# Rope's cosine product on VectorE, late steps of the q chain one by one, and two in three of the second head's exponential sums on VectorE

## The chip, the cores and the metric

The kernel runs on one core of a Trainium2 chip. The time is device microseconds (us) of one execution, the median of three runs: 2183.52 us for the kernel before. The engines are named as the profile names them: PE (TensorE; PEld is its loading of weights), DVE (VectorE), ACT (ScalarE), POOL (GpSimd) and SP (SyncE, which issues the transfers). Each engine works through its own queue in order; an instruction that waits holds up all that stands behind it in that queue.

## The reference, cut to what matters

```python
for i in range(DEPTH):                       # DEPTH = 2 layers, 1040 positions x 1024 channels
    hn = rmsnorm(h, norm_w[i])
    proj = einsum("bld,de->ble", hn, w_in[i])
    (u_pool, g_pool, u_fft, g_fft, xbc, z, dt_raw, q, k, v, g_attn) = split(proj, points)
    y_pool = multiscale_pool(...) * silu(g_pool)
    y_fft = fourier_mix(...) * silu(g_fft)
    y_ssd = ssd_mixer(...)
    y_att = gqa_axial(q, k, v, ...) * silu(g_attn)
    h = h + einsum("ble,ed->bld", concatenate([y_pool, y_fft, y_ssd, y_att]), w_out[i])

def gqa_axial(q, k, v, q_norm_w, k_norm_w, cos, sin):   # 8 query heads, 2 key heads, 64 wide
    q = rope2d(rmsnorm(q, q_norm_w), cos, sin)
    k = rope2d(rmsnorm(k, k_norm_w), cos, sin)
    s = einsum(q, k) * scale
    p = softmax(s, axis=-1)
    return einsum(p, v)
```

The change lies in the rope of q and k, and in the denominators of the softmax.

## The kernel before

Everything is kept with channels on the 128 partitions and positions along the columns. The 1040 positions are cut into three chunks `CH` of 348, 346 and 346 columns (332 for the first in layer 1), and the keys into nine tiles `KTS` of 116 (112 for the last).

**Projections.** `proj` computes one tile of 128 output channels: for each chunk 8 x 3 matmuls (`mm3`, lines 133 to 135: high part times high, high times low, low times high), with a `yield` after every second of the eight groups, so four steps a chunk (`PC = 4`). It then calls `evac` on the PSUM tile. If `evac` is a generator, its first part runs before the last `yield` of the chunk; with `QS = 1` all that is left of it runs at once at the start of the next step, ahead of the next chunk's matmuls. Weights come in by `wraw` (line 198) and are split in `split`: ACT writes the high part (129), DVE the low part (130).

**The q and k chain, `qk_chunk`, the body of `evac` for these tiles.** ACT copies the projection out of PSUM (528) and squares it (530), then a `yield`; PE sums the squares over each head (533), `rstd` makes the inverse root in three ACT and three DVE instructions (139 to 146), DVE multiplies with it (535) and swaps neighbours (537), SP loads the cosines (539) and sines (540), POOL multiplies with the cosines (541), DVE multiplies the swapped copy with the sines (542) and adds the two (543). `att_q` then writes the result's high and low parts (ACT 585, DVE 586), `att_kv` those of the key tile (558 to 560). There are 30 such chunks: 2 layers x (1 key tile + 4 query tiles) x 3 chunks. Their small tiles come from a ring of four (`smq`).

**Attention.** `att_max` finds an upper bound of each query's scores: 27 or so matmuls per head (605) and a DVE maximum of each (606), in some 20 steps; the negated maxima are brought across by POOL's memset (609), PE transposes (616) and ACT copies (618). `att_main` goes through three chunks of queries with nine key tiles each; `score` does, for the two heads `e` = 0, 1 of a tile `t`, two matmuls (634, 635), the exponential on ACT (637), and adds the exponentials of successive key tiles up on POOL (644 for key tiles 0 and 1, 646 for the others). `weigh` multiplies with v (656), `divide` turns the sums into the quotients (665 to 671). An exponential's tile (`pf`, 14 buffers) is free when both `weigh` and its sum have read it.

**What runs beside what.** `weave` interleaves generators: each has a nominal number of steps, and the next step is taken from the one that is least far along. For query tile `t` it weaves `att_main(t)` (38 + 12 steps), `att_q(t+1)` and `att_max(t+1)` (20 + 12 steps) and a part of `fill`, a chain of the other projections and their side work (`FO`; "D" is the SSD step sizes `ssd_dt`, lines 708 to 744, and `pool_group` works in lines 695 and 696). Ahead of that stand, in program order, `prenorm`, `att_kv`, whose two streams (the key and the value projection) take four steps by turns, and `fft_tables` (lines 392 to 420: loads of `fw`, DVE additions 407 and 411, matmuls 415). After attention come the output projections and the SSD scans, which the change doesn't touch.

The order within each engine's queue is not the program's: a planner sets it when the program is built, from the program's order and from its own estimate of when each instruction could start. So instructions of neighbouring steps pass each other.

Of the kernel before, what the change touches and what calls it, by code (L numbers as in the profile page):

```python
# [14 lines left out]
ALU = mybir.AluOpType  # L15
# [37 lines left out]
def hybrid_trunk(ctx: ExitStack, tc: tile.TileContext, io, out, depth=DEPTH):  # L53
    nc = tc.nc
# [28 lines left out]
    PC = 8 // GK  # L83
# [3 lines left out]
    LS = 38  # L87
    QS = 1
    OS = (7, 8)
# [62 lines left out]
    def vec(l, col, n=1):  # L152
        return vecs[:, l * NV + col:l * NV + col + n]
# [47 lines left out]
    def proj(s, w, evac, cols=128, ch=CH):  # L201
        for ci, (c0, cw) in enumerate(ch):
            p = ps("mm")
            for k in range(8):
                mm3(p[:cols, :cw], *w[k], s.hh[k][:, c0:c0 + cw], s.hl[k][:, c0:c0 + cw], k == 0, k == 7)
                if k % GK == GK - 1 and k < 7:
                    yield
            late = evac(ci, c0, cw, p[:cols, :cw])
            late = late if isgenerator(late) else iter(())
            if QS:  # L210
                next(late, None)
                yield
            for _ in late:
                pass
            if not QS:
                yield

# [308 lines left out]
    def qk_chunk(l, s, wcol, c0, cw, p):  # L526
        raw = sm("q")
        nc.scalar.copy(raw[:, :cw], p)
        sq = sm("q")
        nc.scalar.activation(sq[:, :cw], raw[:, :cw], AF.Square)  # L530
        yield
        ss = ps("xx")
        nc.tensor.matmul(ss[:, :cw], blk, sq[:, :cw], start=True, stop=True)
        rs = rstd(ss[:, :cw], cw, 64, "q")
        nc.vector.scalar_tensor_tensor(raw[:, :cw], raw[:, :cw], vec(l, wcol), rs[:, :cw], op0=ALU.mult, op1=ALU.mult)
        sw = sm("q")
        nc.vector.stream_shuffle(sw[:, :cw], raw[:, :cw], [i ^ 1 for i in range(32)])
        cos, sin = sm(), sm()
        nc.sync.dma_start(cos[:, :cw], io["cosT"][:, c0:c0 + cw])
        nc.sync.dma_start(sin[:, :cw], io["sinT"][:, c0:c0 + cw])  # L540
        nc.gpsimd.tensor_tensor(raw[:, :cw], raw[:, :cw], cos[:, :cw], op=ALU.mult)
        nc.vector.tensor_tensor(sw[:, :cw], sw[:, :cw], sin[:, :cw], op=ALU.mult)
        nc.vector.tensor_tensor(raw[:, :cw], raw[:, :cw], sw[:, :cw], op=ALU.add)
        return raw

    def att_kv(l, s):
# [16 lines left out]
        for _ in CH:  # L563
            for g in streams:
                yield from islice(g, PC)
        yield from chain(*streams)
# [54 lines left out]
    def att_main(l, s, t):  # L621
# [5 lines left out]
        def score(c0, cw, k):  # L627
# [4 lines left out]
            for e in range(2):  # L632
# [5 lines left out]
                pfs.append(pf)  # L638
            for e, pf in enumerate(pfs):
                if k == 0:  # L640
                    first[e] = pf
                elif k == 1:
                    accs[c0, e] = phase["p"].tile([128, 348], F32, name=nm("acc"), tag="acc", bufs=NACC)
                    nc.gpsimd.tensor_tensor(accs[c0, e][:n, :cw], first[e][:n, :cw], pf[:n, :cw], op=ALU.add)
                else:
                    nc.gpsimd.tensor_tensor(accs[c0, e][:n, :cw], accs[c0, e][:n, :cw], pf[:n, :cw], op=ALU.add)  # L646
            return pfs
# [332 lines left out]
    for l in range(depth):  # L980
# [29 lines left out]
        phase["spare"] = SPARE[1]  # L1010
        run(weave((chain(att_q(l, s, 0), att_max(l, s, 0)), 3 * PC + 17), (islice(fill, FN[0] * PC), FN[0] * PC)))
        for t in range(4):
# [5 lines left out]
            if t < 3:  # L1018
                run(weave((att_main(l, s, t), LS + 3 * PC), (chain(*side), 20 + 3 * PC), (islice(fill, n), n)))
        d0, d1, d2 = [hidden() for _ in range(3)]  # L1020
# [134 lines left out]
```

## Time and profile before

| | |
|---|---|
| median of 3 runs | 2183.52 us (2173.6 to 2186.84) |
| the profiled execution | 2183.98 us, of which the span is 2181.9 us |
| PE busy | 2002.1 us, 92% of the span |
| DVE busy | 1323.7 us, 61% |
| ACT busy | 1004.6 us, 46% |
| POOL busy | 642.0 us, 29% |
| granted TensorE clock, mean | 0.964 |

A profile shows one execution. A row of the timeline gives start, duration, engine, line, operation, the tile written and those read, how many instructions are merged in it, and in brackets how long the engine stood idle before it and what ended that. A row of the waits gives an engine and line, what it waited for, the total, the number of times and the longest. In a row of the windows, PEclk is the granted clock as a share of 2.4 GHz.

### The profile page before, as it was taken

What the parts mean: (1) busy time and instruction counts of PE and PEld (TensorE: products, weight loads), DVE (VectorE), ACT (ScalarE), POOL (GpSimd) and SP (SyncE); (2) the same over time, 40 slices, a digit from 0 to 9 for tenths busy, and PEclk for the clock granted to TensorE, in tenths of its full rate; (3) what the DMA queues carried; (4) which work ended last, traced back from release to release, by engine and by line L of the source; (5) the groups of instructions that cost most, each with busy time, mean ns of one, the idle gap of its engine ahead of it and who ended that gap; (6) DMA issues with size and microseconds to landing.
All of it is one profiled execution on the core that took longest, in us unless ns stands there. A gap on an engine that the chain in (4) does not pass through costs nothing. (4 is left out here: it accounts for less than half of the span.)

```text
span 2181.9 us, 33618 instructions
## 1 busy us (share of the span) xinstructions
PE 2002.1 (92%) x11868; PEld 1755.1 (80%) x11868; DVE 1323.7 (61%) x2614; ACT 1004.6 (46%) x2191; POOL 642.0 (29%) x642
## 2 busy tenths in 40 slices
PE   6699999989999999988976999999999999988888
PEld 5498888867899868877864988888778997878778
DVE  6373535558566355689864735256576554466996
ACT  5335254444443456346443353444435425463562
POOL 3005235135131220245220142441442304112550
PEclk9799999999999999999997999999999999999999
DMA  4321222113224478776743212121223335776666
GB/s 131 103 86 61 59 66 74 36 56 95 94 81 137 126 217 267 195 186 187 223 125 108 88 59 68 64 63 34 76 81 99 124 113 149 246 231 179 176 190 188
DMA packets 170374, 269.48 MB, mean 124 GB/s; under 512 B 21522, under 2 KB 117334, under 8 KB 170206
## 3 DMA queue, kind: packets, MB, share of 16 engines
q1 hardware_dynamic: 167550, 258.01, 39.0%
q0 software_dynamic: 2656, 9.33, 1.7%
q8 instruction: 93, 1.52, 0.3%
q14 instruction: 75, 0.61, 0.1%
HBM read 189.27 MB, written 73.77 MB: 121 GB/s over the span
## 5 line engine op out<-in xcount | busy, mean ns | idle before, releaser
L133 PE MATMUL psmm<-big,wh 128*128 128x346 f32 (+2 forms) x1920 | 639.8, 333 | 27.0 <-ACT sms L334 9.2
L134 PE MATMUL psmm<-big,wh 128*128 128x346 f32 (+2 forms) x1920 | 629.7, 328 | 7.7 <-DVE big L130 4.0
L135 PE MATMUL psmm<-big,wl 128*128 128x346 f32 (+2 forms) x1920 | 626.3, 326 | 2.0 <-DVE wl L130 2.0
L646 POOL TENSOR_TENSOR acc<-acc,pf 116x346 f32<-116x346 f32 (+4 forms) x336 | 343.9, 1048 | 531.6 <-ACT pf L637 531.5
L133 PEld LDWEIGHTS psmm<-big,wh 128*128 128x128 f32 x1920 | 367.9, 192 | 62.2 <-issue 21.7
L134 PEld LDWEIGHTS psmm<-big,wh 128*128 128x128 f32 x1920 | 368.2, 192 | 19.5 <-DVE big L130 8.4
L135 PEld LDWEIGHTS psmm<-big,wl 128*128 128x128 f32 x1920 | 368.3, 192 | 6.3 <-DVE wl L130 2.6
L130 DVE TENSOR_TENSOR wl<-wr,wh 128x512 fp32r<-128x512 f32 x232 | 182.8, 792 | 215.2 <-ACT wh L129 214.2
L129 ACT CAST wh<-wr 128x512 fp32r<-128x512 f32 (+1 forms) x236 | 145.0, 616 | 270.9 <-PE psmm L134 216.7
L133 PE MATMUL psy<-big,wh 128*128 128x346 f32 (+2 forms) x672 | 224.1, 334 | 0.0
L134 PE MATMUL psy<-big,wh 128*128 128x346 f32 (+2 forms) x672 | 223.1, 332 | 1.1 <-POOL big L182 0.7
L135 PE MATMUL psy<-big,wl 128*128 128x346 f32 (+2 forms) x672 | 219.2, 326 | 0.0
L606 DVE TENSOR_REDUCE mx<-psy 128x1 f32<-128x346 f32 (+3 forms) x272 | 132.8, 512 | 56.1 <-PE psy L605 55.4
L637 ACT ACTIVATE pf<-psy 116x346 f32<-116x346 f32 (+4 forms) x288 | 125.6, 457 | 80.3 <-PE psy L635 77.2
L656 PE MATMUL pspv<-pf,vt 116*64 116x346 f32 (+5 forms) x864 | 160.6, 463 | 0.0
L133 PEld LDWEIGHTS psy<-big,wh 128*128 128x128 f32 x672 | 129.9, 193 | 10.9 <-issue 8.8
L134 PEld LDWEIGHTS psy<-big,wh 128*128 128x128 f32 x672 | 130.0, 193 | 8.5 <-DVE big L130 2.8
L135 PEld LDWEIGHTS psy<-big,wl 128*128 128x128 f32 x672 | 130.3, 194 | 1.3 <-issue 0.8
L606 DVE TENSOR_REDUCE mx<-pssc 128x1 f32<-128x346 f32 (+3 forms) x136 | 69.9, 514 | 69.3 <-PE pssc L605 68.4
L337 DVE TENSOR_TENSOR sms<-sms,psmm 128x346 f32<-128x346 f32 (+2 forms) x128 | 65.1, 511 | 73.7 <-PE psmm L135 43.8
L656 PEld LDWEIGHTS pspv<-pf,vt 116*64 116x64 f32 (+1 forms) x864 | 58.6, 136 | 61.5 <-issue 24.0
L634 PE MATMUL psy<-big,big 128*116 128x346 f32 (+4 forms) x288 | 95.8, 334 | 8.1 <-DVE mx L606 7.2
(285 smaller groups left out, 3331.3 us busy)
## 6 DMA issues: line engine op xcount, KB each, us to landing
wr<-w SPq DMA_DIRECT2D x248, 256.0 KB
hd<-sms SPq DMA_DIRECT2D x112, 173.0 KB
sms<-hd SPq DMA_DIRECT2D x112, 173.0 KB
bb<-csd SPq DMA_DIRECT2D x40, 338.0 KB
md<-big SPq DMA_DIRECT2D x24, 520.0 KB
gd<-sms SPq DMA_DIRECT2D x64, 173.0 KB
big<-gd SPq DMA_DIRECT2D x16, 520.0 KB
big<-md SPq DMA_DIRECT2D x16, 520.0 KB
```

The source lines that it names most:

```text
L129: nc.scalar.copy(hi, src)
L130: nc.vector.tensor_tensor(lo, src, f(hi), op=ALU.subtract)
L133: nc.tensor.matmul(out_ps, ah, bh, start=start, stop=False)
L134: nc.tensor.matmul(out_ps, ah, bl, start=False, stop=False)
L135: nc.tensor.matmul(out_ps, al, bh, start=False, stop=stop)
L337: nc.vector.tensor_tensor(ht, ht, p[:, :cw], op=ALU.add)
L606: nc.vector.tensor_reduce(mx[:qn, q, e, ci:ci + 1], p[:qn, :cw], axis=AX.X, op=ALU.max)
L634: nc.tensor.matmul(p[:n, :cw], k1[:, k0:k0 + n], s1[e][:, cs], start=True, stop=False)
L637: nc.scalar.activation(pf[:n, :cw], p[:n, :cw], AF.Exp, scale=0.125)
L646: nc.gpsimd.tensor_tensor(accs[c0, e][:n, :cw], accs[c0, e][:n, :cw], pf[:n, :cw], op=ALU.add)
L656: nc.tensor.matmul(hold["pv"][64 * e:64 * e + 64, :cw], s.vt[:n, k, v, :], pfs[e][:n, :cw], start=(k == 0), stop=(k == len(KTS) - 1))
```

## The change

The generator in `proj` hands on every `yield` of `evac` as a step of its own, and `qk_chunk` has two more: one after `rstd`, one at its end. The nominal step numbers grow with that (6 more for the 3 chunks of a query tile; in `att_kv` the key stream takes six steps by turns with four of the value stream). The cosine product moves from POOL to DVE, and so do the sums of head `e` = 1 for the key tiles `k` = 1, 2, 4, 5, 7 and 8.

```diff
-    QS = 1
...
             late = evac(ci, c0, cw, p[:cols, :cw])
             late = late if isgenerator(late) else iter(())
-            if QS:
-                next(late, None)
-                yield
-            for _ in late:
-                pass
-            if not QS:
-                yield
+            next(late, None)
+            yield
+            yield from late
...
         rs = rstd(ss[:, :cw], cw, 64, "q")
+        yield
         nc.vector.scalar_tensor_tensor(raw[:, :cw], raw[:, :cw], vec(l, wcol), rs[:, :cw], op0=ALU.mult, op1=ALU.mult)
...
-        nc.gpsimd.tensor_tensor(raw[:, :cw], raw[:, :cw], cos[:, :cw], op=ALU.mult)
+        nc.vector.tensor_tensor(raw[:, :cw], raw[:, :cw], cos[:, :cw], op=ALU.mult)
         nc.vector.tensor_tensor(sw[:, :cw], sw[:, :cw], sin[:, :cw], op=ALU.mult)
         nc.vector.tensor_tensor(raw[:, :cw], raw[:, :cw], sw[:, :cw], op=ALU.add)
+        yield
         return raw
...
         for _ in CH:
-            for g in streams:
-                yield from islice(g, PC)
+            for g, n in zip(streams, (PC + 2, PC)):
+                yield from islice(g, n)
...
             for e, pf in enumerate(pfs):
+                eng = nc.vector if e == 1 and k % 3 else nc.gpsimd
                 if k == 0:
                     first[e] = pf
                 elif k == 1:
                     accs[c0, e] = phase["p"].tile([128, 348], F32, name=nm("acc"), tag="acc", bufs=NACC)
-                    nc.gpsimd.tensor_tensor(accs[c0, e][:n, :cw], first[e][:n, :cw], pf[:n, :cw], op=ALU.add)
+                    eng.tensor_tensor(accs[c0, e][:n, :cw], first[e][:n, :cw], pf[:n, :cw], op=ALU.add)
                 else:
-                    nc.gpsimd.tensor_tensor(accs[c0, e][:n, :cw], accs[c0, e][:n, :cw], pf[:n, :cw], op=ALU.add)
+                    eng.tensor_tensor(accs[c0, e][:n, :cw], accs[c0, e][:n, :cw], pf[:n, :cw], op=ALU.add)
...
-        run(weave((chain(att_q(l, s, 0), att_max(l, s, 0)), 3 * PC + 17), (islice(fill, FN[0] * PC), FN[0] * PC)))
+        run(weave((chain(att_q(l, s, 0), att_max(l, s, 0)), 3 * PC + 6 + 18), (islice(fill, FN[0] * PC), FN[0] * PC)))
...
-                run(weave((att_main(l, s, t), LS + 3 * PC), (chain(*side), 20 + 3 * PC), (islice(fill, n), n)))
+                run(weave((att_main(l, s, t), LS + 3 * PC), (chain(*side), 20 + 3 * PC + 6), (islice(fill, n), n)))
```

## Rows read from the trace of the kernel before

**Rows 1.** The page's first part: busy time, share of the span and instructions of each engine.

```profile
span 2181.9 us, 33618 instructions
PE 2002.1 (92%) x11868; PEld 1755.1 (80%) x11868; DVE 1323.7 (61%) x2614; ACT 1004.6 (46%) x2191; POOL 642.0 (29%) x642
```

**Rows 2.** Busy time in the two stretches in which attention is woven with the projections (layer 0, layer 1): length, then busy us and instructions of PE, PEld, DVE, ACT and POOL, granted clock, DMA share, GB/s.

```profile
100.00:850.00 750.00, 727.36 (x4273) 634.72 (x4273) 417.92 (x777) 340.94 (x705) 222.27 (x223) 0.99 0.32 101
1195.00:1880.00 685.00, 664.69 (x3957) 581.51 (x3956) 376.87 (x700) 306.08 (x649) 217.08 (x220) 0.99 0.29 91
```

**Rows 3.** PE's own waits in the same two stretches, the longest, and the larger of those for DVE; first layer 0, then layer 1: total us, times, longest. The rows of L606 and of L669 read the same in both layers and stand once.

```profile
PE psmm L133 <- ACT big L759: 4.3, 1, 4.3
PE psy L634 <- DVE mx L606: 3.6, 3, 1.5
PE psxx L748 <- DVE big L744: 2.4, 1, 2.4
...
PE psxx L533 <- DVE smn L669: 1.1, 1, 1.1
...
PE psmm L133 <- ACT big L759: 4.5, 1, 4.5
PE psxx L748 <- DVE big L744: 4.5, 3, 3.7
```

**Rows 4.** POOL's timeline around PE's longest wait of each stretch.

```profile
471.61 14.96 POOL L646 TENSOR_TENSOR acc<-acc,pf 116x348 f32<-116x348 f32 x14
486.53 0.91 POOL L541 TENSOR_TENSOR smq<-smq,smn 128x348 f32<-128x348 f32 x1
...
1552.65 14.41 POOL L646 TENSOR_TENSOR acc<-acc,pf 116x332 f32<-116x332 f32 x14
```

**Rows 5.** DVE, ACT and PE behind the first of them.

```profile
481.66 0.55 DVE L542 TENSOR_TENSOR smq<-smq,smn 128x348 f32<-128x348 f32 x1
487.48 0.52 DVE L543 TENSOR_TENSOR smq<-smq,smq 128x348 f32<-128x348 f32 x1 [5.26 <-POOL smq L541]
488.03 0.98 ACT L585 CAST big<-smq 64x348 fp32r<-64x348 f32 x2 [5.12 <-DVE smq L543]
490.20 0.43 ACT L759 COPY big<-psmm 128x348 f32<-128x348 f32 x1
490.68 0.66 PE L133 MATMUL psmm<-big,wh 128*128 128x346 f32 x1 [4.26 <-ACT big L759]
```

**Rows 6.** The windows of 12 us over the two stalls, with an undisturbed one between; columns as in rows 2.

```profile
486.00:498.00 12.00, 7.74 (x31) 6.89 (x31) 9.10 (x12) 6.95 (x14) 7.12 (x6) 0.72 0.11 44
500.00:512.00 12.00, 12.00 (x75) 10.06 (x75) 9.29 (x11) 7.61 (x17) 9.33 (x7) 1.00 0.17 52
1566.00:1578.00 12.00, 7.45 (x36) 6.40 (x36) 8.65 (x12) 6.93 (x14) 7.58 (x7) 0.72 0.11 45
```

**Rows 7.** Groups of instructions by line: count, busy us, mean ns of one, idle time of the engine before them.

```profile
L646 POOL TENSOR_TENSOR acc<-acc,pf 116x346 f32<-116x346 f32 (+4 forms) x336 | 343.9, 1048 | 531.6 <-ACT pf L637 531.5
L541 POOL TENSOR_TENSOR smq<-smq,smn 128x346 f32<-128x346 f32 (+2 forms) x30 | 33.2, 1108 | 171.8 <-DVE smq L537 138.8 <-PE psmm L133 20.3 <-ACT wh L129 6.9
L542 DVE TENSOR_TENSOR smq<-smq,smn 128x346 f32<-128x346 f32 (+2 forms) x30 | 23.2, 774 | 0.5
L543 DVE TENSOR_TENSOR smq<-smq,smq 128x346 f32<-128x346 f32 (+2 forms) x30 | 17.9, 596 | 22.8 <-POOL smq L541 22.5
```

**Rows 8.** Shortest, median and longest duration (ns) of two of these lines, the sine product on DVE and the sums on POOL.

```profile
L542 DVE TENSOR_TENSOR smq<-smq,smn x30: 503/522/1249, 56.7 to 1603.0; 128x346 f32<-128x346 f32 x20, 128x348 f32<-128x348 f32 x6, 128x332 f32<-128x332 f32 x4
L646 POOL TENSOR_TENSOR acc<-acc,pf x336: 882/933/1949, 168.2 to 1858.4; 116x346 f32<-116x346 f32 x96, 116x348 f32<-116x348 f32 x24, 116x332 f32<-116x332 f32 x24, 112x346 f32<-112x346 f32 x16
```

**Rows 9.** POOL and DVE side by side in layer 0, where PE then waits 1.5 us for a maximum.

```profile
221.96 4.67 POOL L646 TENSOR_TENSOR acc<-acc,pf 116x346 f32<-116x346 f32 x4 [1.09 <-ACT pf L637]
...
222.19 1.14 DVE L146 TENSOR_TENSOR smq<-smq,smq 128x346 f32<-128x346 f32 x1
...
224.59 1.24 DVE L535 SCALAR_TENSOR_TENSOR smq<-smq,vecs,smq 128x346 f32<-128x346 f32 x1
225.76 0.51 DVE L606 TENSOR_REDUCE mx<-psy 116x1 f32<-116x348 f32 x1
```

**Rows 10.** The start of layer 0: DVE, PE and the transfer queue around the tables' additions.

```profile
64.66 9.32 SPq L402 DMA_DIRECT2D big<-fw  x1
73.65 0.69 DVE L407 TENSOR_TENSOR big<-big,big 128x512 f32<-128x512 f32 x1 [9.78 <-DMA big<-fw]
74.26 0.57 DVE L535 SCALAR_TENSOR_TENSOR smq<-smq,vecs,smq 128x346 f32<-128x346 f32 x1
75.47 1.52 PE L533 MATMUL psxx<-smq,ct 128*128 128x346 f32 x2 [8.48 <-ACT smq L530]
87.92 2.04 PE L415 MATMUL psy<-big,big 128*128 128x512 f32 x2 [8.32 <-issue]
```

**Rows 11.** The loads of the sines and cosines in layer 1: SP's issue of a load of cosines, and the first product with the sines that are loaded right behind it.

```profile
1191.10 0.38 SPq L539 DMA_DIRECT2D smn<-cosT  x1
...
1200.73 0.50 DVE L542 TENSOR_TENSOR smq<-smq,smn 128x332 f32<-128x332 f32 x1
```

## The prediction

> **What bounds the kernel now.** I read the page's busy times first: PE is busy for 92% of the span and no other engine for over 61% [rows 1]. The change adds no matmul and takes none away, so it can only win back time in which PE stands still or runs at the lower clock, and can only lose by making PE wait. Second, windows over the two stretches of woven attention, where nearly all of the edits act: 750 us with PE busy for 727, and 685 us with 665 [rows 2]. The reader is to see how little is left: 23 and 20 us of idle time, and what the clock loses after an idle spell. Third, PE's own waits there: the longest in each layer is the same one, 4.3 and 4.5 us for ACT's copy at line 759; then come waits for DVE, of which L606, L744 and L669 make 7.1 us in layer 0 and 9.2 in layer 1, 16.3 together [rows 3].
>
> Fourth, the timelines under that longest wait. POOL has fallen behind: it does 14 sums in one run, 14.96 us in layer 0 and 14.41 in layer 1, and only then the cosine product [rows 4]. DVE was done with the sine product at 482.2 and waits 5.26 us for POOL; ACT's cast at 585 stands 5.12 us behind DVE; the copy at 759, which would free a PSUM bank, stands behind that cast in ACT's queue; and PE waits 4.26 us for it [rows 5]. POOL, busy for 29% of the span, is on the path here. Fifth, the price, from windows of 12 us: 31 and 36 matmuls start over the two stalls, where an undisturbed window starts 75, or 6.25 per us, and the granted clock has a mean of 0.72 instead of 1.00, so part of the window runs at 1.2 GHz [rows 6]. 31 matmuls are worth 5.0 us and 36 are worth 5.8, so the stalls cost 7.0 and 6.2 us: **13.3 us**, clock included.
>
> **The change part by part.**
>
> *Cosine product on DVE.* 30 instructions leave POOL (33.2 us, 1108 ns each). On DVE the nearest rows are the products before and behind it, of the same shape: 774 ns on the mean where POOL works beside it, 596 where it rarely does [rows 7]. With 600 ns DVE gets 18 us more, 14 of them in the 24 query chunks. DVE no longer hands the chunk to POOL and back: 18 waits, 22.5 us [rows 7], of which the two stalls hold about 10.3. Without POOL in the chain those two stalls cannot arise in this form: **-13.3 us**. Of the other 12.2 us most lies beside a busy PE; bounds 0 to 12.2, I take **-2**, by PE's two waits of 1.1 us behind the chain [rows 3].
>
> *Sums of the second head.* Six of eight per chunk and query tile, 2 layers x 4 tiles x 3 chunks x 6 = 144 of 384, leave POOL (about 1.05 us each, 151 us in all). On DVE such a sum isn't in the trace. From below the shortest two-input product, 0.50 us, from above the longest, 1.25 [rows 8]: 72 to 180 us. I take the mean of the sine product, 0.77, since it too runs beside POOL's instruction: 111 us. What DVE does in the two stretches grows from 418 + 377 = 795 us [rows 2] to 795 + 111 + 14 = 920, from 55% to 64% of 1435 us. In most places this is covered by PE's own work. What isn't covered are PE's 16.3 us of waits for DVE. If these grow with DVE's load (x 1.16) that is +2.6 us; if with busy over free time (1.24 to 1.79, x 1.44), +7.2. I take **+4**, nearer the first, since POOL's instructions, beside which DVE is slow, become fewer. Without that cover each sum could cost PE its 0.77 us, 111 us in all.
>
> What a DVE sum waits for: the exponential on ACT, and for k = 4 and 7 POOL's sum of the tile before, on the same accumulator; 48 such hand-offs. Behind it in DVE's queue stand maxima (606), for whose PSUM banks the score matmuls wait, and the low parts of weights (130).
>
> What the rows show of DVE beside POOL: with four sums on POOL, two DVE instructions over as many columns as a sum take 1.14 and 1.24 us, and the maximum that PE is waiting for comes after them [rows 9]. The Trainium skill ("SBUF — State Buffer", section "SBUF: two separate sides") says that VectorE and GpSimd share one pair of ports as an exclusive lock, and that an instruction of two SBUF inputs blocks, or is blocked, for the other's whole duration; the rows agree in kind. By that rule as an estimate each moved sum would take up to 0.50 + 0.93 = 1.43 us, 206 us in all instead of 111; this goes into the second rival.
>
> *Late steps one by one.* No instruction is added. Into the first new step go PE's head sums (533), three ACT and three DVE instructions; into the second DVE's multiply, swap, products and add and SP's two loads; into the third two ACT casts, two DVE subtractions, and only then the next chunk's first six matmuls. So a chunk's end passes up to two steps of the other streams, on ACT the copies and exponentials among them, which is right: ACT's cast no longer stands ahead of other tiles' copies before its input is near. For SP the loads move behind the weights that a step of `fill` issues; they were issued 9.6 us ahead of their use [rows 11], so I take nothing; if late, DVE now waits where POOL did. In `att_kv` the head sums now directly follow the key's matmuls instead of four steps of the value's; if the planner found nothing in between, PE would see ACT's copy and square (about 1 us) six times, +6. Against that stands the start of layer 0, where PE waits 8.48 us for a square whose buffer DVE frees only behind the tables' addition (407), itself waiting 9.78 us for a load [rows 10]; the key's multiply (535) misses getting ahead of that addition by one place in DVE's queue. Bounds +6 to -8.5; I take **0**, because PE next waits for the tables at 87.92 anyway [rows 10], which this change doesn't bring forward.
>
> **The sum.** -13.3 - 2 + 4 + 0 = -11.3 us on the profiled execution's 2183.98 (span 2181.9, 2.1 around it; 0.46 above the median of the three runs): 2172.7, said as **2173 us**.
>
> **The rivals.**
>
> *1. More is won.* If the key's chain gets ahead of the tables' addition (-8.5) and all of the 12.2 us of hand-backs shows on PE, with +4 for DVE: 2184 - 13.3 - 12.2 - 8.5 + 4 = 2154, some 2150 with the lower clock avoided there. For: the key's multiply misses by one place. Against: PE's next wait for the tables. Chance 0.25.
>
> *2. DVE's queue is held up (slower than before).* Each of the 48 hand-offs holds DVE for one POOL sum of 0.93 us [rows 8]; where `att_max` is woven in, about half, PE waits for the maxima behind: 24 x 0.93 = 22 us, with +7.2 for the load: 2184 - 15.3 + 29.5 = 2198. It decides once the 144 sums cost PE over 15.3 us, 0.11 us apiece; from 0.26 apiece the kernel is over 1% slower. For: rows 9. Against: POOL is idle for 531.6 us before its sums, waiting for ACT [rows 7], so it is rarely behind. The port lock named above, as this kernel would feel it, works the same way: 795 + 206 + 14 = 1015 us on DVE, 71%, busy over free 2.42, x 1.95, +15.5, and 2184. Chance 0.25 together.
>
> *3. The stall only moves.* Scores still come in a burst there, and POOL still has 10 of 16 sums a chunk, about 10 us; if PE then waits for a PSUM bank behind exponentials or DVE sums as long as now behind the cast: 2184. Chance 0.1.
>
> The forecast, 2162 to 2184, has 0.4.
>
> **How the numbers follow.** 1%, 22 us, is about what a measurement of this kernel can tell from no change. Faster by over 1% (under 2162): rival 1 and a little of the forecast's own tail, 0.28. Slower (over 2205): the upper part of rival 2, 0.08. Within: 0.64. The range goes from rival 1's 2150, a little lowered to 2148, to rival 2's 2198; outside lie the ends of both, some 0.18.
>
> **What would show it.** Right: no 4 us wait of PE for line 759; DVE's sums near 0.8 us; POOL near 640 - 184 = 456 us and DVE near 1450; PE's waits for L606 under 12 us; the waits at the tables as before. Wrong: idle time of DVE ended by POOL's sums, with PE's waits for L606 or 130 behind it; DVE sums over 1.2 us; PE idle ahead of 533 in `att_kv`; or tables that start earlier.

## The result and the profile after

The changed kernel takes 2155.11 us (median of 4 runs, 2153.69 to 2159.7) against 2185.18 us of the kernel before beside it on the same chip: ratio 0.987, 95% interval 0.9847 to 0.9894. Measured once more it took 2152.92 us, ratio 0.9885 (0.9856 to 0.9914). The change makes the kernel faster by some 1.2 to 1.3%, 23 to 30 us, where 11 were forecast.

The page's busy lines after the change, which answer to [rows 1]:

```profile
PE 1987.1 (92%) x11868; PEld 1752.6 (81%) x11868; DVE 1396.0 (65%) x2788; ACT 1003.9 (47%) x2191; POOL 454.8 (21%) x468
```

POOL fell to 455 us, as forecast (456). DVE grew by 72 us, not by the 129 that the prediction added up. Windows over the two stretches of woven attention, for [rows 2]:

```profile
100.00:827.00 727.00, 711.68 (x4258) 626.93 (x4256) 452.06 (x864) 338.36 (x699) 130.03 (x139) 1.00 0.33 104
1170.00:1848.00 678.00, 663.92 (x3955) 584.18 (x3954) 414.95 (x784) 305.22 (x649) 126.98 (x136) 0.99 0.29 92
```

DVE does 867 us here (forecast 920), and PE stands idle for 15.3 and 14.1 us instead of 23 and 20. Why DVE grew so little stands in the groups by line (count, busy us, mean ns, idle time before), for [rows 7]. New line numbers: sums 642 and 644, cosine, sine product and addition 537 to 539, and 144 is one of the three DVE steps of `rstd`.

```profile
L644 POOL TENSOR_TENSOR acc<-acc,pf 116x346 f32<-116x346 f32 (+5 forms) x216 | 213.5, 1001 | 691.5 <-ACT pf L634 618.4 <-DVE wl L129 47.9 <-DVE big L756 11.8
...
L644 DVE TENSOR_TENSOR acc<-acc,pf 116x346 f32<-116x346 f32 (+5 forms) x120 | 108.8, 906 | 72.1 <-ACT pf L634 53.4 <-POOL acc L644 17.3
...
L642 DVE TENSOR_TENSOR acc<-pf,pf 116x346 f32<-116x346 f32 (+2 forms) x24 | 20.8, 866 | 40.0 <-ACT pf L634 39.9
...
L538 DVE TENSOR_TENSOR smq<-smq,smn 128x346 f32<-128x346 f32 (+2 forms) x30 | 16.1, 535 | 0.2 <-DMA smn<-sinT 0.2
...
L537 DVE TENSOR_TENSOR smq<-smq,smn 128x346 f32<-128x346 f32 (+2 forms) x30 | 15.5, 516 | 0.8
```

The 144 sums take 129.6 us, 0.90 each, more than the 111 forecast, and DVE waits 17.3 us for POOL's sum of the same accumulator. But the sine product came down from 774 ns to 535. DVE has 145 us of new work (sums and 15.5 us of cosine products) and is busy for only 72 us longer: all its other instructions together became 73 us shorter.

PE's waits for a maximum (7.2 us of `psy` and 0.8 of `pssc` before) and the two of over 4 us for line 759 (now 757) are gone. Two of the lines that say what PE waits for now, in all (total, times, longest), for [rows 3]:

```profile
PE psy L410 <- issue: 36.1, 2, 18.3
...
PE psy L631 <- ACT pf L634: 6.4, 4, 3.6
```

The first and longest, the tables at the start of the layers, was there before with 27.6 us. The second (0.9 us before) is new in this size: a score matmul waits for an exponential, since its PSUM bank is still to be read. The longest of these, in layer 1, has the form of the old stall of [rows 5]; ACT, DVE and PE there:

```profile
1542.95 0.45 ACT L656 COPY big<-pspv 128x332 f32<-128x332 f32 x1
1547.57 0.98 ACT L582 CAST big<-smq 64x346 fp32r<-64x346 f32 x2 [4.17 <-DVE smq L539]
1548.58 0.81 ACT L634 ACTIVATE pf<-psy 116x346 f32<-116x346 f32 x2
...
1547.02 0.52 DVE L539 TENSOR_TENSOR smq<-smq,smq 128x346 f32<-128x346 f32 x1
...
1549.09 0.64 PE L631 MATMUL psy<-big,big 128*116 128x346 f32 x1 [3.61 <-ACT pf L634]
```

ACT's cast of the query chunk still stands at the head of ACT's queue before its input is there, 4.17 us, with two exponentials behind it; PE waits 3.61 us. The chain's products now run on DVE alone.

**Where the time went.** Since both kernels run the same 11,868 matmuls, the traces can be laid on each other by the count of matmuls: the time from the start of one to the start of another, in us. "Stall 0" and "stall 1" are the 200 matmuls from the 2400th and from the 8300th on, wide enough to hold what a variant leaves of the two stalls: in the kernel before, PE's waits come ahead of the 2472nd and the 8399th matmul, after the change (now for an exponential) ahead of the 2518th and the 8445th. "First queries" is 400 to 1200 and 6400 to 7000, where `att_q` and `att_max` of the first tile are woven with `fill`. "Other attention" is the rest of 400 to 4400 and 6400 to 10000; "after it" is 4400 to 6400, in which layer 1 begins, and everything from 10000.

| trace | first 400 | first queries | stall 0 | stall 1 | other attention | after it |
|---|---|---|---|---|---|---|
| before | 119.6 | 232.0 | 44.0 | 43.0 | 999.4 | 729.1 |
| before, second trace | 116.7 | 233.5 | 44.1 | 42.9 | 1000.9 | 730.7 |
| after | 112.9 | 226.8 | 37.3 | 42.2 | 989.7 | 728.7 |
| after, second trace | 116.6 | 226.8 | 37.3 | 42.1 | 991.3 | 723.1 |
| cosine product alone | 117.8 | 229.9 | 41.2 | 41.4 | 992.1 | 724.0 |
| steps alone | 117.6 | 230.5 | 41.5 | 42.3 | 994.0 | 728.5 |
| sums alone | 116.8 | 230.7 | 42.0 | 38.8 | 998.6 | 724.1 |
| cosine and steps | 114.5 | 227.5 | 37.2 | 41.0 | 991.0 | 728.1 |
| sums left out | 114.8 | 226.8 | 34.9 | 36.0 | 979.7 | 728.6 |
| all 384 sums on DVE | 114.5 | 226.8 | 34.1 | 35.4 | 979.5 | 726.4 |

The four attention columns repeat within some 1.6 us between two traces of one program, the first and the last only within 4 and 6. By them the change wins 7.5 us in the stalls, nearly all of it in layer 0, 5 to 7 in the first queries and 10 in the other attention, together some 22 to 24. The rest lies in columns that scatter as much as they differ.

### The profile page after: what moved, and what is told of

It reads as the page before. It is cut to its first block, busy times and chain, and to the rows that moved or that the text cites. A ratio compares the mean times of both kernels' runs of the same rounds, so it can differ in the third digit from the quotient of the medians.

```text
span 2151.9 us, 33411 instructions
## 1 busy us (share of the span) xinstructions
PE 1987.1 (92%) x11868; PEld 1752.6 (81%) x11868; DVE 1396.0 (65%) x2788; ACT 1003.9 (47%) x2191; POOL 454.8 (21%) x468
## 5 line engine op out<-in xcount | busy, mean ns | idle before, releaser
L644 POOL TENSOR_TENSOR acc<-acc,pf 116x346 f32<-116x346 f32 (+5 forms) x216 | 213.5, 1001 | 691.5 <-ACT pf L634 618.4
L129 DVE TENSOR_TENSOR wl<-wr,wh 128x512 fp32r<-128x512 f32 x232 | 168.2, 729 | 137.4 <-ACT wh L128 136.6
L132 PE MATMUL psy<-big,wh 128*128 128x346 f32 (+2 forms) x672 | 222.9, 332 | 0.0
L133 PE MATMUL psy<-big,wh 128*128 128x346 f32 (+2 forms) x672 | 218.0, 324 | 1.1 <-POOL big L181 0.8
L644 DVE TENSOR_TENSOR acc<-acc,pf 116x346 f32<-116x346 f32 (+5 forms) x120 | 108.8, 906 | 72.1 <-ACT pf L634 53.4
L603 DVE TENSOR_REDUCE mx<-psy 116x1 f32<-116x346 f32 (+3 forms) x272 | 132.7, 511 | 23.6 <-PE psy L602 23.0
L132 PEld LDWEIGHTS psy<-big,wh 128*128 128x128 f32 x672 | 127.6, 190 | 13.0 <-issue 10.0
L133 PEld LDWEIGHTS psy<-big,wh 128*128 128x128 f32 x672 | 127.6, 190 | 6.7 <-issue 1.6
```

Of the source, the lines that this page charges most:

```text
L129: nc.vector.tensor_tensor(lo, src, f(hi), op=ALU.subtract)
L132: nc.tensor.matmul(out_ps, ah, bh, start=start, stop=False)
L133: nc.tensor.matmul(out_ps, ah, bl, start=False, stop=False)
L603: nc.vector.tensor_reduce(mx[:qn, q, e, ci:ci + 1], p[:qn, :cw], axis=AX.X, op=ALU.max)
L644: eng.tensor_tensor(accs[c0, e][:n, :cw], accs[c0, e][:n, :cw], pf[:n, :cw], op=ALU.add)
```

## The experiments

Each variant has the planner's order for its own edit, so it differs in more than the edited lines. Ratios are to the kernel before in the same series, with their 95% interval.

**The parts alone.** Cosine product alone:

```diff
-        nc.gpsimd.tensor_tensor(raw[:, :cw], raw[:, :cw], cos[:, :cw], op=ALU.mult)
+        nc.vector.tensor_tensor(raw[:, :cw], raw[:, :cw], cos[:, :cw], op=ALU.mult)
```

> The kernel before with the cosine product alone on DVE. Theory A (port relief: with fewer sums on POOL DVE's other instructions get shorter, so PE stops waiting for DVE; the stalls are worth 12 us, the rest of the 30 us lies in those waits and in the layers' starts): the two stalls of 4.3 and 4.5 us are gone, PE's waits for the maxima stay near 8 us, DVE busy +15 to +18; 2171, about -13. Rival B (the spread steps bring the rest): the same here, 2171. Rival C (the rest comes from the key chain at a layer's start, through the product on DVE): the start of layer 0 is some 7 us earlier too, 2163.

Sums alone:

```diff
+                eng = nc.vector if e == 1 and k % 3 else nc.gpsimd
...
-                    nc.gpsimd.tensor_tensor(accs[c0, e][:n, :cw], accs[c0, e][:n, :cw], pf[:n, :cw], op=ALU.add)
+                    eng.tensor_tensor(accs[c0, e][:n, :cw], accs[c0, e][:n, :cw], pf[:n, :cw], op=ALU.add)
```

> The kernel before with the 144 sums alone on DVE, cosine product on POOL. Theory A: POOL's runs of 14 sums become runs of 10, the stalls shrink to about 1 us each, DVE busy rises by 60 instead of the 130 us that the sums take, the sine product falls from 774 to about 560 ns, PE's waits for the maxima fall below 3 us; 2165, -20. Rival B: stalls gone, but the waits for the maxima stay or grow; 2175. Rival C: 2172 with no change in the layers' starts.

Late steps alone (the edits in `proj`, `qk_chunk`, `att_kv` and the two nominal step numbers):

```diff
         rs = rstd(ss[:, :cw], cw, 64, "q")
+        yield
...
+        yield
         return raw
```

> The kernel before with the late steps alone spread (both yields, the step numbers, the turns in the key and value projections). Theory A: DVE waits for POOL as before, the stalls are shortened at most by half since ACT's cast no longer stands ahead of other copies, the waits for the maxima stay near 8 us; 2178, -6. Rival B: -15 to -20, with the waits for the maxima gone. Rival C: the start of layer 0 earlier by 5 to 7 us, 2172.

Cosine product and late steps, the sums left as before:

> The changed kernel with all sums back on POOL. Theory A: the stalls are gone, but without the relief for DVE the waits for the maxima stay at 4 to 8 us; 2168, 13 above the changed kernel. Rival B: 2157, as the changed kernel, since sums bring nothing. Rival C: 2160.

Measured: cosine 0.9914 (0.9896 to 0.9932), sums 0.9946 (0.9924 to 0.9969), steps 0.9951 (0.9932 to 0.9969), cosine and steps 0.9878 (0.9855 to 0.9901). Cosine and steps do what the whole change does; the sums, worth 12 us alone, are worth nothing on top. Of the theories, A falls as it stands and B comes nearest. Each part alone takes only a piece of the 87.0 us of the two stall columns (cosine 4.4, sums 6.2, steps 3.2; the whole change 7.5, all sums on DVE 17.5). With the cosine product alone PE meets the next wait in the same place, in layer 0 and in layer 1 (its own line numbers):

```profile
PE psy L634 <- ACT pf L637: 3.2, 1, 3.2
...
PE psy L634 <- ACT pf L637: 3.1, 1, 3.1
```

The two remaining pairs, cosine with sums and steps with sums (the same edits):

> The full change without the spread late steps. Measured alone, the cosine product brought -18.8 us, the sums -13.1, the spread steps -9.9; cosine and steps together -27.4, all three -30. Theory P (the parts free the same waits: cosine and sums both keep the rope chain from standing behind POOL's sums, the steps alone keep it from standing behind ACT's and DVE's queues): about 2162, ratio 0.991, no better than the cosine product alone, and PE's wait for an exponential of some 3 us at 470 and 1550 us still there. Rival R (each part gains in its own places, fewer sums on POOL make DVE faster everywhere): -18.8 - 13.1 = -32, 2149, ratio 0.985. Rival L (a floor at about -29 that any two parts reach): 2153.

> The full change with the cosine product left on POOL. Theory P: sums shorten what the chain stands behind on POOL, steps the rest, so the two add up as cosine and steps did: -9.9 - 13.1 = -23, about 2158, ratio 0.9895; the stalls at 470 and 1550 us nearly gone, as with cosine and steps. Rival R says the same -23. Rival L: 2153. If steps and sums free the same wait: -13, 2168.

Measured 0.9919 (0.9889 to 0.9949) and 0.9917 (0.9888 to 0.9945). The sums add nothing once the cosine product is on DVE, and some 7 us to the steps while it is on POOL. The times are nearest to theory P, but its sign is not there: with cosine product and sums on DVE PE's wait of 3 us for an exponential is gone in both layers, and the two stall columns fall from 82.6 to 77.0 us. What the sums win there PE loses elsewhere (the other attention takes 995.3 us instead of 992.1). So theory P's reason, that both parts free the same wait, is not shown.

**The start of the layers.** The full change, but the key's late steps drained as before:

```diff
+        def held(*x):
+            g = evac(*x)
+            next(g)
+            yield
+            for _ in g:
+                pass
...
-        streams = [proj(s, win(l, T_K), evac), proj(s, win(l, T_V), lambda ci, c0, cw, p: nc.scalar.copy(vt[:, c0:c0 + cw], p))]
+        streams = [proj(s, win(l, T_K), held), proj(s, win(l, T_V), lambda ci, c0, cw, p: nc.scalar.copy(vt[:, c0:c0 + cw], p))]
-            for g, n in zip(streams, (PC + 2, PC)):
+            for g, n in zip(streams, (PC, PC)):
```

> The full change, but the key's chunks are drained in one step as before and the turns between key and value are as before; only the query chunks have spread steps. Theory C (the start of the layers is part of the gain: by the curve of matmuls -7 us in layer 0, about -3 in layer 1): -30 + 10 = -20, about 2161; the tables' first matmul at 87.9 us as before. Rival (the curve's first 7 us are mostly scatter of one profile, or come from the cosine product): 2154, ratio 0.987 to 0.988.

Measured 0.9867 (0.9831 to 0.9903), the same as the full change: the steps in `att_kv` do nothing, theory C falls. A second trace of the kernel before (it took 2185.61 us) and one of the full change:

> The kernel before once more, for a second trace: how far two traces of the same program differ at the same matmul. If the first 400 matmuls end within 1 us of the first trace's 130.0, the 7 us that the changed kernel is ahead there are its own; if they end near 126 to 127, some 3 of them are scatter, which every variant showed.

> The full change once more, beside the other three on the same chip: 2155, ratio 0.987 as before. Its trace, laid on the first, shows what of the gain over the first 400 matmuls (7.2 us) and of the tables' wait is scatter of single traces.

The 400th matmul comes at 126.9 us in the second trace of before (first 130.0), at 126.7 in the second of after (first 122.9). PE's idle time over these matmuls is 26.2 and 26.3 us in before's two traces and the same two values in after's; PE's busy time for them differs, and the granted clock, whose mean from 10 us to there is 0.84 and 0.87 in before's traces, 0.89 and 0.85 in after's. The window of the second trace of before:

```profile
10.00:127.00 117.00, 90.58 (x401) 70.22 (x402) 66.95 (x130) 56.69 (x124) 22.20 (x21) 0.87 0.33 108
```

What looked like a gain of 7 us at the start is scatter of single traces, for the most part.

**Which of the two new stops.** On the kernel with the cosine product on DVE, only the stop after the inverse root (first), or only the one at the chain's end (second):

```diff
         rs = rstd(ss[:, :cw], cw, 64, "q")
         yield                      # only in cos_first
...
         yield                      # only in cos_second
         return raw
```

> Cosine product on DVE, and of the two new stops in a chunk's late work only the first: head sums and their root in one step; rope, casts and subtractions together in the next. Cosine product alone: ratio 0.9914; with both stops 0.9878. Theory F (the gain comes from letting the rope chain start in a step of its own): 0.988, 2156. Theory S (it comes from the casts' own step): 0.991, 2164, and PE's wait for exponentials of about 3 us stays at 470 and 1550 us.

> Cosine product on DVE, and of the two new stops only the second: head sums, root and rope together in one step, casts and subtractions in the next. Theory S: 0.988, 2156, PE's wait for exponentials at 470 and 1550 us as short as with both (about 2 and 3.6 us). Theory F: 0.991, 2164. If both single stops come out near 0.9895, each gives half.

Measured 0.9908 (0.9872 to 0.9943) and 0.9902 (0.9871 to 0.9933). By medians neither theory. The count of matmuls tells more: either stop alone takes all of the stalls' gain (the two stall columns are 76.7 us with either, 78.2 with both and 82.6 with none), but in the first queries either loses 4 us of it again (234.0 and 234.1 against 229.9 with none and 227.5 with both). These variants also have smaller nominal step numbers, which move the weave; why the first queries suffer was not tried.

**The wait that is left.** The full change with the query's casts on DVE:

```diff
-                nc.scalar.copy(hi, src)
+                nc.vector.tensor_copy(hi, src)
```

> The full change, and the two casts of each query chunk go from ACT to DVE (48 instructions of 0.5 us, 24 us more on DVE). Theory Q (the wait of 3.6 us that is left in layer 1 and 2.1 in layer 0 is the old one in new clothes: ACT's cast waits for the rope chain on DVE with exponentials behind it in ACT's queue): these two waits for exponentials go, about -6 us and -3 for the clock after them: 2146, ratio 0.983. Rival (DVE is the slower engine by now, its 24 us cost as much as is won): 2155, ratio 0.987.

Measured 0.9894 (0.9871 to 0.9917), no better than the full change. The wait for exponentials in layer 0 went as theory Q said (no idle time between the 2400th and 2600th matmul, 34.5 us instead of 37.3), but in the next 200 PE met a new one behind DVE's longer queue:

```profile
PE psy L631 <- DVE mx L603: 5.3, 1, 5.3
```

Layer 1 does the same: 35.7 us for stall 1 instead of 42.2, and then 3.8 us of waiting for a maximum.

**What the sums cost.** The 144 sums on DVE left out:

```diff
             for e, pf in enumerate(pfs):
-                eng = nc.vector if e == 1 and k % 3 else nc.gpsimd
+                eng = nc.gpsimd
+                if e == 1 and k % 3:
+                    continue
...
```

> The full change with the 144 sums of the second head that it puts on DVE left out (the second head is divided by the first head's sums, so the output is not the reference's). It gives what the full change would bring if these sums cost nothing on either engine. Theory N (with cosine and steps in place the sums neither help by leaving POOL nor cost on DVE): 2154, within 2 us of the full change's 2155. Rival X (they cost what the prediction said, +4, and their leaving POOL brings about as much): 2150 or below. Upper bound on their price: the prediction's 0.77 us apiece, 111 us on DVE, of which PE would see at most what this run is faster by.

Measured 0.9789 (0.9757 to 0.9821), 2133.95 us. N falls, and X has the side right and the size far too small: by the ratios it is 18 us below the full change, 0.12 us for each sum; in the table 8.6 us of it lie in the stalls and 10 in the other attention. Since the same sums on POOL are no cheaper, what they cost on either engine had to be told apart:

```diff
+                cs_ = 8 if e == 1 and k % 3 and k > 1 else cw
...
-                    eng.tensor_tensor(accs[c0, e][:n, :cw], accs[c0, e][:n, :cw], pf[:n, :cw], op=ALU.add)
+                    eng.tensor_tensor(accs[c0, e][:n, :cs_], accs[c0, e][:n, :cs_], pf[:n, :cs_], op=ALU.add)
...
```

> The full change with the 144 sums of the second head left on DVE in number, place and waits, but 120 of them (all but each chunk's first) over 8 columns instead of 346 (1 is added before the logarithm so that it has no zero; the output is not the reference's). With the sums left out the kernel took 0.979 of before's time, with them 0.987 on DVE and 0.988 on POOL: about 17 us on either engine. Theory D (what costs is the time that the sums take on their engine, and what stands behind them there): most of it comes back, ratio about 0.980, 2139. Rival W (what costs is the instruction itself, its place, its waits for exponentials and POOL's sums, or the order that it brings about): 2152 or more, ratio 0.986 to 0.987.

> Cosine product on DVE and spread steps as in the full change, but the sums of the second head stay on POOL; 120 of the 144 that the change would move go over 8 columns instead of 346 (1 added before the logarithm; the output is not the reference's). Ratio with whole sums on POOL: 0.988. Theory D (time on the engine: on POOL a sum takes 1.0 us and makes DVE's instructions beside it longer): about as with short sums on DVE, ratio 0.980, 2139, and DVE's other instructions some 40 us shorter in all than with whole sums on POOL. Rival W: 0.986 to 0.988, 2152 to 2155. If DVE's instructions get shorter and the time stays, DVE's speed beside POOL is not on PE's path.

Measured: short on DVE 0.9835 (0.9808 to 0.9862), short on POOL 0.9807 (0.9781 to 0.9833). On POOL theory D holds. On DVE the result lies between, and the durations say why (count, then shortest, median and longest in ns): first POOL's whole sums, then DVE's short ones.

```profile
L645 POOL TENSOR_TENSOR acc<-acc,pf x216: 887/932/2027, 164.4 to 1827.0; 116x346 f32<-116x346 f32 x64, 116x348 f32<-116x348 f32 x16, 116x332 f32<-116x332 f32 x16, 112x346 f32<-112x346 f32 x8
L645 DVE TENSOR_TENSOR acc<-acc,pf x120: 139/695/903, 164.8 to 1827.3; 116x8 f32<-116x8 f32 x96, 112x8 f32<-112x8 f32 x24
```

An addition of 8 columns takes 139 ns at the least and 695 at the median. It is held up, and by what, the timeline shows:

```profile
553.53 1.98 POOL L645 TENSOR_TENSOR acc<-acc,pf 116x346 f32<-116x346 f32 x2 [30.73 <-ACT pf L634]
...
553.84 0.65 DVE L645 TENSOR_TENSOR acc<-acc,pf 116x8 f32<-116x8 f32 x1 [2.35 <-ACT pf L634]
...
555.98 0.15 DVE L645 TENSOR_TENSOR acc<-acc,pf 116x8 f32<-116x8 f32 x1
```

POOL adds up the first head's exponentials from 553.53 on, two sums in 1.98 us; DVE's sum of the same key tile starts 0.31 us later and ends at 554.49, about where the first of the two ends. At 555.98 POOL is done, and the same addition takes 0.15 us. So it is throughout: of the 120 short sums 83 run beside a sum on POOL, and 82 of these end 21 to 28 ns behind it; the 35 that run beside no POOL instruction take 139 to 168 ns. The Trainium skill ("SBUF — State Buffer", section "SBUF: two separate sides") calls the ports that VectorE and GpSimd share an exclusive lock, which whoever starts first keeps for its whole instruction; these rows agree.

**None on POOL.** If the two engines hold each other up, the cure is not two thirds of one head's sums on DVE but all of both heads':

```diff
-                eng = nc.vector if e == 1 and k % 3 else nc.gpsimd
+                eng = nc.vector
```

> The full change with all 384 sums on DVE and none on POOL. DVE gets 240 more. Theory D1 (DVE and POOL hold each other up: an 8-column sum on DVE took 139 ns at the least but 695 at the median, beside POOL's sum of the other head): with none on POOL a sum takes DVE about 0.51 us instead of 0.91 and DVE's other instructions get shorter, DVE's busy time near 1400 + 240 x 0.51 - 144 x 0.4 - some 60 = 1405 us, and the time stays near the full change: 2150 to 2158. Rival D2 (DVE's queue is what PE feels: 240 x 0.51 us = 122 us more ahead of maxima and of the rope chain): at the 0.12 us a sum measured so far +29 us, 2184 or more, with PE waiting for the maxima again.

Measured 2130.93 us (2127.3 to 2132.76), ratio 0.9783 (0.9753 to 0.9813): 22 us faster than the full change beside it, faster than either theory said. DVE's busy time is 1407.9 us for 240 more sums, against 1396.0 after the change. Its sums of line 644:

```profile
L644 DVE TENSOR_TENSOR acc<-acc,pf x336: 484/515/530, 163.0 to 1806.2; 116x346 f32<-116x346 f32 x96, 116x348 f32<-116x348 f32 x24, 116x332 f32<-116x332 f32 x24, 112x346 f32<-112x346 f32 x16
```

and those of the change itself:

```profile
L644 DVE TENSOR_TENSOR acc<-acc,pf x120: 488/1032/1253, 162.0 to 1825.9; 116x346 f32<-116x346 f32 x64, 116x348 f32<-116x348 f32 x16, 112x346 f32<-112x346 f32 x16, 116x332 f32<-116x332 f32 x16
```

Not one of 336 is longer than 530 ns; of the change's 120 the median is 1032. All 384 sums take 186 us on DVE, its 144 took 129.6. The windows over attention with all sums on DVE:

```profile
100.00:820.00 720.00, 711.10 (x4259) 626.35 (x4258) 458.40 (x979) 336.55 (x699) 10.00 (x19) 1.00 0.33 104
1165.00:1829.00 664.00, 657.48 (x3956) 578.74 (x3955) 421.32 (x904) 304.54 (x649) 8.26 (x16) 1.00 0.29 93
```

DVE is as busy as after the change (880 against 867 us), and PE idles for 15.4 us instead of 29.4. The Trainium skill ("GPSIMD Engine Reference", section "4.1 Engine selection") puts elementwise additions on VectorE, GpSimd being about half as fast with two inputs; here the medians are 933 ns on POOL [rows 8] and 515 on DVE, a factor of 1.8. Does this one edit do it all? The kernel before, with it alone:

```diff
+                eng = nc.vector
...
-                    nc.gpsimd.tensor_tensor(accs[c0, e][:n, :cw], first[e][:n, :cw], pf[:n, :cw], op=ALU.add)
+                    eng.tensor_tensor(accs[c0, e][:n, :cw], first[e][:n, :cw], pf[:n, :cw], op=ALU.add)
...
-                    nc.gpsimd.tensor_tensor(accs[c0, e][:n, :cw], accs[c0, e][:n, :cw], pf[:n, :cw], op=ALU.add)
+                    eng.tensor_tensor(accs[c0, e][:n, :cw], accs[c0, e][:n, :cw], pf[:n, :cw], op=ALU.add)
```

> The kernel before with all 384 sums on DVE, the cosine product still on POOL and the late steps as before. Theory D1 (POOL's sums held up DVE and the rope chain; without them the chain finds POOL idle): most of the gain with one edit, ratio 0.980 to 0.984, 2139 to 2148, sums at 0.52 us. Rival K (the cosine product and the steps are needed as they were for the sums of one head, which alone gave 0.9946): the parts add up as 0.978 / 0.988, ratio 0.990, 2160.

Measured 2141.67 us, 0.9827 (0.98 to 0.9855), by medians a larger gain than the whole change; DVE's waits for POOL's cosine product fell from 22.5 us to 9.7. The other two parts bring another 10 us or so (0.9783). And is it the pairing that hurts? The full change with as many sums on DVE, chosen by key tile:

```diff
-                eng = nc.vector if e == 1 and k % 3 else nc.gpsimd
+                eng = nc.vector if k % 3 == 2 else nc.gpsimd
```

> The full change with the same number of sums on DVE (144), but both heads' sums of three key tiles in eight instead of six in eight of the second head's: the two sums of one tile now go to the same engine. Theory B (the pair released at one time to two engines is what collides): DVE's sums come down from 0.91 us to about 0.6, and the time towards the middle between the full change and all on DVE, ratio 0.983, 2146. Rival (any sum on POOL beside any two-input work on DVE costs the same): DVE's other instructions lose what the sums win, ratio 0.987, 2155.

Measured 0.9845 (0.9819 to 0.9871), 2147.82 us. Most of DVE's sums have their own duration now:

```profile
L644 DVE TENSOR_TENSOR acc<-acc,pf x144: 475/511/1250, 163.5 to 1820.8; 116x346 f32<-116x346 f32 x64, 112x346 f32<-112x346 f32 x32, 116x348 f32<-116x348 f32 x16, 116x332 f32<-116x332 f32 x16
```

The median went from 1032 to 511 ns: 32 of these 144 sums run beside a POOL instruction, of the change's 120 it was 87. So it was mostly the pair, released at one time, that collided. The time points to theory B, but its interval overlaps the full change's. And DVE still waits 22.7 us in all for POOL's sum of the same accumulator, as it does for 17.3 us in the full change. With all sums on DVE these hand-offs are gone together with the collisions; what each of the two costs PE was not told apart.

## Why the prediction was right or wrong

The direction was right, and 2155 us lies in the range of 2148 to 2198, but the forecast of 2173 won less than half of what was measured, and its "within 1%" (0.64) was the wrong side of the line. By the ratios the cosine product brought 19 us where 15.3 were forecast, the late steps on top of it 8 where nothing was, and the sums on top of both nothing where a loss of 4 was. Point by point:

**The stalls, -13.3: too large by nearly half, since one of them only moved.** They gave 7.5 us, 6.7 in layer 0 and 0.8 in layer 1. The step said that without POOL in the chain the stalls "cannot arise in this form". That holds literally, and yet ACT's cast stands in ACT's queue as before, waiting for DVE instead. In layer 1 PE's wait comes 46 matmuls later and is 3.61 us long instead of 4.5. The 12 us over it, for [rows 6]:

```profile
1545.00:1557.00 12.00, 8.39 (x39) 8.10 (x38) 8.60 (x15) 6.00 (x12) 3.63 (x4) 0.72 0.08 23
```

39 matmuls start here, 36 did before, at the same mean clock of 0.72; by the prediction's own count of 6.25 per us this stall still costs 5.8 us, against 6.2. That is the third rival, "the stall only moves" (0.1), for one of the two stalls. In layer 0 the cosine product alone won 2.8 us, with a wait of 3.2 us for an exponential left over, and the steps another 4.0.

**Late steps, 0: this step failed.** "I take 0" rested on the layers' start, and there it was right: the key's multiply did get ahead of the tables' addition, as the first rival had it, and won nothing. DVE and PE at the start of layer 0, for [rows 10]:

```profile
60.74 0.56 DVE L531 SCALAR_TENSOR_TENSOR smq<-smq,vecs,smq 128x346 f32<-128x346 f32 x1
...
82.02 0.69 DVE L402 TENSOR_TENSOR big<-big,big 128x512 f32<-128x512 f32 x1 [9.01 <-DMA big<-fw]
...
84.91 2.04 PE L410 MATMUL psy<-big,big 128*128 128x512 f32 x2 [17.77 <-issue]
```

The multiply runs at 60.74, PE's wait of 8.48 us for a square is gone, and PE waits 17.77 us at the tables instead, whose addition DVE does when its load has landed. What the step left out is the query chunks, for which the prediction had the mechanism in words ("ACT's cast no longer stands ahead of other tiles' copies") and no number. On top of the cosine product the steps gave 8 us, 4.0 of them in the stall of layer 0 and 2.4 in the first queries.

**DVE's sums, +4, taken between 2.6 and 7.2: this step failed, by what it left out.** It let PE's 16.3 us of waits for DVE [rows 3] grow with DVE's load. They fell to 6.0 us: of the three lines only 744 (now 742) is left, and the maxima and line 669 are gone. In layer 0, then in layer 1:

```profile
PE psxx L746 <- DVE big L742: 2.6, 1, 2.6
...
PE psxx L746 <- DVE big L742: 3.4, 2, 3.1
```

The price of a sum on DVE was too low (0.77 us, measured 0.90), and as a whole the 144 sums do cost PE about 18 us, 0.12 apiece, more than the 0.11 from which the second rival was to decide. The kernel did not become slower, as that rival had it, because the same sums cost about as much on POOL. Short sums on POOL show that: 0.9807 against 0.9878, 11 us by the traces and 15 by the medians' ratios. The prediction saw POOL "idle for 531.6 us before its sums", counted that as slack, and took no gain on PE into account: it priced DVE's slowness beside POOL for the moved sums, and not what PE was already paying for sums where they were. The sum of both is nothing: 0.9878 without this part of the change, 0.987 and 0.9885 with it.

**Other hand-backs, -2 with bounds 0 to -12.2: too small.** The 2 us were read from PE's two waits of 1.1 us "behind the chain", but these are for line 669, which belongs to `divide` and not to the rope chain. The first queries gained 5 to 7 us and the other attention 10. PE's waits for maxima went from 8.0 us to none, where the list asked for under 12: 3.0 of them were in the first queries, one of 1.5 us in each layer, the case of [rows 9], and 4.9 in the other attention. Each part of the change alone lowers them (to 5.8 us with the cosine product, 4.2 with the sums, 2.6 with the steps). They are about half of what these two columns gained. Of the other half no single wait was followed up.

**The rivals.** More is won (0.25) had nearly the right time, 2154, by a wrong sum: its 8.5 us at the layers' start do not exist, and of its 13.3 for the stalls 7.5 came. DVE's queue held up (0.25) had a real mechanism: DVE waits 17.3 us in all for POOL's sums, and in the kernel with the casts on DVE PE does wait 5.3 us for a maximum. The port lock's estimate, 1.43 us a sum, was too high (0.90), but the rule behind it mattered more than its price: it speaks against sharing one job between the two engines, and the best kernel doesn't.

**What stays open.** The two pairs of traces differ by 30 and 32 us, and some 8 us of that are not in the attention columns. In the first pair they lie mostly in the first 400 matmuls, in the second after attention, where two traces of one program differ by up to 4 and 6 us; whether the change wins anything there is not shown.

## What to carry to other kernels

An engine's idle share does not make its work free: POOL was idle for 71% of the span, and taking its 384 sums away won more, by medians, than the whole change. Work that two engines share should not be split within pairs that are released together; try the whole of it on one engine first, and look at the shortest and the median duration of one instruction, which lie far apart where two engines hold each other up. When a stall is taken apart, ask of each edit alone what PE waits for next in that place, and look some way behind it: one of the two stalls here only moved by 46 matmuls and cost nearly as much as before.

## What the runs showed of the hardware

An addition of 8 columns on DVE took 139 to 168 ns with nothing beside it on POOL and up to 903 beside a POOL addition, and in 82 of 83 cases it ended 21 to 28 ns behind that addition. DVE instructions with one input from SBUF are held up too; here is `rstd`'s line 144, one input, shortest, median and longest in the changed kernel and with all sums on DVE:

```profile
L144 DVE TENSOR_SCALAR smq<-smq x30: 265/558/1033, 39.9 to 1568.0; 128x346 f32<-128x346 f32 x20, 128x348 f32<-128x348 f32 x6, 128x332 f32<-128x332 f32 x4
```

```profile
L144 DVE TENSOR_SCALAR smq<-smq x30: 265/335/343, 40.0 to 1555.4; 128x346 f32<-128x346 f32 x20, 128x348 f32<-128x348 f32 x6, 128x332 f32<-128x332 f32 x4
```

The maxima of line 603, whose input is in PSUM, are not: in these two kernels they took 511 and 513 ns on the mean. And with every sum on DVE, a busier DVE (66% of the span against 61% before) cost PE less than a shared POOL.
